# Two transformer blocks on one core: both feed-forward networks by a seven-product block scheme instead of plain products

## The chip, the core and the metric

The kernel runs on one NeuronCore of a Trainium2 chip. The core has a matrix engine (TensorE, PE in the profile, with its weight loads shown apart as PEld), a vector engine (VectorE, DVE), an activation engine (ScalarE, ACT), a general engine (GpSimd, POOL) and a queue that issues transfers (SyncE, SP). SBUF is the on-chip memory that all of them read; PSUM is where TensorE leaves its products. The metric is the device time of one execution in microseconds. Before the change it is 1985.58 us, the median of three runs (1983.51 to 1989.43).

## The reference

One batch of 512 tokens with 1024 features goes through two transformer blocks in float32. Only the feed-forward networks are touched by the change. They are

```
hffn = modulate(rmsnorm(x, g_norm2[l]), shift2, scale2)
a, u = jnp.split(jnp.einsum('bsd,df->bsf', hffn, w_ffn_in[l]), 2, axis=-1)
x = x + gate2[:, None, :] * jnp.einsum('bsf,fd->bsd', jax.nn.silu(a) * u, w_ffn_out[l])
...
h = rmsnorm_2(x, norm_ffn[l])
x = x + (jax.nn.silu(h @ w_ffn_gate[l]) * (h @ w_ffn_up[l])) @ w_ffn_down[l]
return rmsnorm_2(x, norm_final)
```

Each network has 2816 hidden features, so it holds a product of 512 x 1024 by 1024 x 5632 and one of 512 x 2816 by 2816 x 1024.

## The kernel before

Float32 accuracy on TensorE comes from a split: every operand is kept as a high part (rounded to the engine's fp32r type by a ScalarE copy) and a low part (the operand minus the high part, on VectorE), and every product is three matmuls, high by high, high by low and low by high (`mm3`, lines 159 to 162). Weights arrive by `weights` (lines 167 to 174): SP loads four row tiles of 256 columns (512 KB) into a `raw` tile, ScalarE writes `wh` (line 172), VectorE writes `wl` (line 173). There are three buffers of each, so loading and splitting run ahead of the matmuls by up to three steps.

A feed-forward network works in 11 stripes of 256 hidden columns (`ffn_hidden`). For each stripe `gemm` runs the gate columns and then the up columns for all 512 tokens: 8 row tiles, 2 column tiles of 128 and 3 matmuls, each streaming 512 columns. PSUM is read by ScalarE (sigmoid, line 869) and VectorE (lines 870 and 873), and the result is split again into the operand of the second product. The second product of the first block goes through `joint`: 22 row tiles by 8 column tiles, feature-major, with the residual update in line 790, the last columns by token halves. That of the second block is token-major: the weights are streamed and the hidden operand is loaded (lines 1352 to 1354), PSUM is started with the transposed residual, and the last norm closes it token tile by token tile (lines 1367 to 1381). The engines run their queues in order; a tile framework lays the buffers out, rotates them per tag, and adds the waits.

GpSimd has little to do in these stretches: it adds squares for the norms (line 799) and issues some spills. In other stretches it also adds and subtracts whole tiles (lines 649, 650, 733, 748), and for part of the second block it makes the low parts of weights (line 173, where `low_engine` is set to it).

## Time and profile before

| what | value |
|---|---|
| median of three runs | 1985.58 us (1983.51 to 1989.43) |
| span of the profiled execution | 1987.4 us |
| TensorE busy | 1919.9 us, 97% |
| VectorE busy | 1060.0 us, 53% |
| ScalarE busy | 732.1 us, 37% |
| GpSimd busy | 318.7 us, 16% |
| first feed-forward network, about | 882 to 1260 us of the span |
| second feed-forward network, about | 1596 us to the end |

The profiled execution has no time of its own beside its span of 1987.4 us, which lies inside the three runs' spread. A share of busy time is an average over the whole span; the stretches differ, and the views by window show each of them. A wait is time in which an engine sat idle before an instruction, with the instruction that released it behind the arrow. The granted clock is TensorE's clock as a share of 2.4 GHz.

### The profile page before, as it was taken

Reading aid. Unit: us, or ns where it says so; the run is one execution under the profiler, and the core shown is the slowest. Engines: PE = TensorE matmul, PEld = TensorE weight load, DVE = VectorE, ACT = ScalarE, POOL = GpSimd, SP = SyncE. Lnnn points to the kernel's source line nnn. Section 1 sums busy time; section 2 is a strip of 40 time slices with the busy share of each in tenths; the row PEclk is TensorE's granted clock in tenths of the full one; section 3 lists DMA queues with packets and bytes.
Section 4 is the critical chain, followed back from the end, with each engine's and each line's share of the span. In section 5 each row is a group of like instructions: output and inputs, shape, how many; then the busy total and the mean of one; then the engine's idle time right before and its main releaser. Section 6 shows DMA issues by size and latency. Waiting matters only on the chain.

```text
span 1987.4 us, 24615 instructions
## 1 busy us (share of the span) xinstructions
PE 1919.9 (97%) x9561; PEld 1574.0 (79%) x9561; DVE 1060.0 (53%) x1730; ACT 732.1 (37%) x1250; POOL 318.7 (16%) x357
## 2 busy tenths in 40 slices
PE   5899999999999999999999999979999999999998
PEld 4677777888989898888888888867877788888886
DVE  6777766645555555654343322587477653443222
ACT  3556654233332323333232223552255532222222
POOL 3322221102030302010000002242344200000000
PEclk7999999999999999999999999989899989999999
DMA  6612222443424243623333234232133123333222
GB/s 210 201 54 64 64 64 78 156 133 96 133 85 144 75 138 118 204 82 96 95 96 95 90 101 122 62 110 64 34 100 101 43 75 95 95 91 92 94 85 74
DMA packets 193521, 199.25 MB, mean 100 GB/s; under 512 B 9719, under 2 KB 178693, under 8 KB 193405
## 3 DMA queue, kind: packets, MB, share of 16 engines
q1 hardware_dynamic: 189920, 188.48, 30.9%
q0 software_dynamic: 3136, 9.08, 1.3%
q8 instruction: 75, 1.23, 0.3%
q14 instruction: 42, 0.34, 0.1%
q10 hardware_dynamic: 348, 0.13, 0.0%
HBM read 189.25 MB, written 9.99 MB: 100 GB/s over the span
## 4 chain that ended last, share of the span: by engine, by line
PE 88%; DVE 6%; ACT 2%; issue 2%; POOL 1%; DMA 1%; SPq 0%; POOLq 0%; DVEq 0%; ACTq 0%
PE ps_g L160 20%; PE ps_g L161 20%; PE ps_g L162 20%; PE ps_g L203 3%; PE ps_g L204 3%; PE ps_g L205 3%; PE ps_o L530 1%; PE ps_z L493 1%; DVE t L319 1%; PE ps_z L161 1%; PE ps_z L160 1%; PE ps_z L162 1%; PE ps_r L515 1%; PE ps_g L1354 1%; PE ps_g L1353 1%
## 5 line engine op out<-in xcount | busy, mean ns | idle before, releaser
L160 PE MATMUL ps_g<-p,wh 128*128 128x512 f32 (+1 forms) x1464 | 584.6, 402 | 11.3 <-ACT p L150 3.0
L161 PE MATMUL ps_g<-p,wh 128*128 128x512 f32 (+1 forms) x1464 | 577.2, 394 | 2.8 <-DVE p L405 2.8
L162 PE MATMUL ps_g<-p,wl 128*128 128x512 f32 (+1 forms) x1464 | 576.2, 394 | 0.0
L173 DVE TENSOR_TENSOR wl<-raw,wh 128x1024 fp32r<-128x1024 f32 (+1 forms) x262 | 325.9, 1244 | 450.8 <-ACT wh L172 449.7
L172 ACT CAST wh<-raw 128x1024 fp32r<-128x1024 f32 (+1 forms) x282 | 294.3, 1044 | 652.5 <-PE ps_g L161 373.1
L160 PEld LDWEIGHTS ps_g<-p,wh 128*128 128x128 f32 x1464 | 276.0, 189 | 83.8 <-issue 14.2
L161 PEld LDWEIGHTS ps_g<-p,wh 128*128 128x128 f32 x1464 | 277.8, 190 | 63.4 <-DVE p L405 3.6
L162 PEld LDWEIGHTS ps_g<-p,wl 128*128 128x128 f32 x1464 | 277.3, 189 | 63.6 <-issue 0.4
L203 PE MATMUL ps_g<-wh,p 128*128 128x256 f32 x512 | 150.4, 294 | 1.5 <-ACT wh L172 1.5
L204 PE MATMUL ps_g<-wl,p 128*128 128x256 f32 x512 | 146.1, 285 | 0.9 <-DVE wl L173 0.9
L205 PE MATMUL ps_g<-wh,p 128*128 128x256 f32 x512 | 145.9, 285 | 0.0
L160 PE MATMUL ps_g<-q,wh 128*128 128x512 f32 (+1 forms) x368 | 142.2, 389 | 0.0
L161 PE MATMUL ps_g<-q,wh 128*128 128x512 f32 (+1 forms) x368 | 141.7, 385 | 0.0
L162 PE MATMUL ps_g<-q,wl 128*128 128x512 f32 (+1 forms) x368 | 141.6, 385 | 0.0
L203 PEld LDWEIGHTS ps_g<-wh,p 128*128 128x128 f32 x512 | 98.9, 193 | 5.3 <-ACT wh L172 1.9
L204 PEld LDWEIGHTS ps_g<-wl,p 128*128 128x128 f32 x512 | 99.2, 194 | 1.7 <-DVE wl L173 1.1
L205 PEld LDWEIGHTS ps_g<-wh,p 128*128 128x128 f32 x512 | 99.1, 193 | 0.0
L160 PEld LDWEIGHTS ps_g<-q,wh 128*128 128x128 f32 x368 | 69.1, 188 | 15.9 <-issue 0.6
L162 PEld LDWEIGHTS ps_g<-q,wl 128*128 128x128 f32 x368 | 69.2, 188 | 15.1
L161 PEld LDWEIGHTS ps_g<-q,wh 128*128 128x128 f32 x368 | 69.2, 188 | 14.6 <-issue 0.2
L150 ACT CAST q<-t 128x512 fp32r<-128x512 f32 (+1 forms) x68 | 39.1, 581 | 87.4 <-DVE t L873 48.7
L319 DVE SCALAR_TENSOR_TENSOR adaacc<-raw,cact,adaacc 128x256 f32<-128x256 f32 x112 | 53.8, 481 | 27.9 <-DMA raw<-in_w_ada 26.1
(373 smaller groups left out, 2622.3 us busy)
## 6 DMA issues: line engine op xcount, KB each, us to landing
raw<-in_w_in SPq DMA_DIRECT2D x108, 512.0 KB, 3.6
raw<-in_w_ffn_in SPq DMA_DIRECT2D x44, 512.0 KB, 3.5
raw<-in_w_ada SPq DMA_DIRECT2D x32, 512.0 KB, 3.4
raw<-in_w_ffn_gate SPq DMA_DIRECT2D x22, 512.0 KB, 3.7
raw<-in_w_ffn_up SPq DMA_DIRECT2D x22, 512.0 KB
raw<-in_w_ffn_down SPq DMA_DIRECT2D x22, 512.0 KB, 3.6
raw<-in_w_ffn_out SPq DMA_DIRECT2D x19, 512.0 KB, 3.5
raw<-in_w_proj_ret SPq DMA_DIRECT2D x16, 512.0 KB, 3.3
```

What stands on the lines that cost most here:

```text
L150: nc.scalar.copy(hi, src)
L160: nc.tensor.matmul(ps, lh, rh, start=start, stop=False)
L161: nc.tensor.matmul(ps, lh, rl, start=False, stop=False)
L162: nc.tensor.matmul(ps, ll, rh, start=False, stop=stop)
L172: nc.scalar.copy(wh, raw)
L173: low_engine["e"].tensor_tensor(out=wl, in0=raw, in1=f(wh), op=ALU.subtract)
L203: nc.tensor.matmul(o, xh[:, ts], wh[:, i], start=k == 0 and t % 2 == 0, stop=False)
L204: nc.tensor.matmul(o, xh[:, ts], wl[:, i], start=False, stop=False)
L205: nc.tensor.matmul(o, xl[:, ts], wh[:, i], start=False, stop=k == KD - 1 and t % 2 == 1)
L319: nc.vector.scalar_tensor_tensor(out=acc, in0=w, scalar=c, in1=acc, op0=ALU.mult, op1=ALU.add)
L493: nc.tensor.matmul(z[:, 0:W], qs[h][r, ts], ks[h][1][r, 0:W], start=False, stop=True)
L515: nc.tensor.matmul(o, src, rhs[:, i * 128:i * 128 + 128], start=True, stop=True)
```

## The change

Both networks are computed by blocks. A block is a 2 x 2 arrangement: the tokens in two halves of 256, the rows of the weight in two halves (four row tiles each, three in the middle group of the second product), and the columns in two halves of 256. In place of 8 half-products per block there are 7 products of sums and differences of quarters; every product is 4 row tiles by 2 column tiles by 3 matmuls that stream 256 columns, 24 matmuls (18 in the middle group). In the first product the two column halves are a gate stripe and its up stripe, so a hidden stripe is one block, and the seven sums of the normed operand (`Operand`, the `S` tiles) are made once and serve all 11 stripes. The second product takes the hidden rows in three groups of 8, 6 and 8 row tiles with two blocks each; for every group seven `S` operands are made anew from the hidden tiles (`hidden_operand`, `sums`).

Per block four differences of weight quarters are made on GpSimd (`sub`: t1 to t4, line 913 of the changed kernel), and seven splits follow where plain products have four (lines 167 and 168). Three partial results are copied from PSUM by ScalarE, and three additions on VectorE put them together. The order of the products is woven over neighbouring blocks (`woven`), and each is prepared two steps ahead (`play`). The second block's second product is now token-major in this form, with its residual transposed during the hidden stripes. Part of SBUF is laid out twice: one set of tags in the mixing stages, another in the feed-forward networks, seven `raw` buffers in place of three among them.

```diff
-# microseconds of weight products traced after each stage of the latency-bound parts
+MIX = {"q": 36, "raw": 3, "wh": 3, "wl": 3}
...
+                return P.tile([128, T], dt, tag=tag, name=tag, bufs=SLOTS[tag])
+            return region["pool"].tile([128, T], dt, tag=tag, name=tag, bufs=region["slots"][tag])
...
+        class Operand:
...
...
+            def put(self, name, piece, src):
+                if name not in self.S:
+                    self.S[name] = [wtile("S", [128, self.kn, 256], F32R) for _ in range(2)]
+                a, n = self.at[piece], self.widths[piece]
+                hi, lo = (x[:, a:a + n] for x in self.S[name])
+                split(src, hi, lo)
...
+            def sums(self, piece, x11, x12, x21, x22, eng=None):
+                eng = eng or nc.gpsimd
+                s1, s2, s3, s4 = (self.temp(piece) for _ in range(4))
+                eng.tensor_tensor(out=s1, in0=x21, in1=x22, op=ALU.add)
+                eng.tensor_tensor(out=s2, in0=s1, in1=x11, op=ALU.subtract)
+                self.put(6, piece, s2)
+                nc.gpsimd.tensor_tensor(out=s3, in0=x11, in1=x21, op=ALU.subtract)
+                self.put(7, piece, s3)
+                self.put(5, piece, s1)
+                nc.gpsimd.tensor_tensor(out=s4, in0=x12, in1=s2, op=ALU.subtract)
+                self.put(3, piece, s4)
+                self.put(4, piece, x22)
...
+                self.kn = len(rows[0])
+                self.raw, self.w, self.ps, self.sb = {}, {}, {}, {}
...
+            def load(self, i, j):
+                t = wtile("raw", [128, self.kn, 256], F32)
+                w, c = self.cols[j - 1]
...
+            def sub(self, out, a, b):
+                nc.gpsimd.tensor_tensor(out=out, in0=a, in1=b, op=ALU.subtract)
+            def prep(self, i):
+                raw = self.raw
+                if i == 1:
+                    self.load(1, 1)
+                elif i == 2:
+                    self.load(2, 1)
+                    src = raw[2, 1]
+                elif i == 6:
+                    self.load(1, 2)
+                    self.load(2, 2)
+                    t1, t3, t4 = raw[1, 1], raw[1, 2], raw[2, 1]
+                    self.sub(t1, raw[1, 2], raw[1, 1])
+                    t2 = wtile("raw", [128, self.kn, 256], F32)
+                    self.sub(t2, raw[2, 2], t1)
+                    self.sub(t3, raw[2, 2], raw[1, 2])
+                    self.sub(t4, raw[2, 1], t2)
+                    self.T = {6: t2, 7: t3, 5: t1, 3: raw[2, 2], 4: t4}
+                    src = t2
+                else:
+                    src = self.T[i]
+                wh = wtile("wh", [128, self.kn, 256], F32R)
+                wl = wtile("wl", [128, self.kn, 256], F32R)
+                split(src, wh, wl)
+                self.w[i] = wh, wl
+            BANK = {1: "A", 6: "A", 5: "A", 3: "A", 2: "B", 7: "C", 4: "C"}
+            TAG = {"A": "g", "B": "z", "C": "r"}
...
+            def product(self, i):
...
+                wh, wl = self.w.pop(i)
+                sh, sl = self.X.S[i]
+                for n in range(2):
+                    o = ps[:, n * 256:n * 256 + 256]
+                    s = slice(n * 128, n * 128 + 128)
+                    for k in range(self.kn):
+                        st = first and n == 0 and k == 0
+                        sp = last and n == 1 and k == self.kn - 1
...
+                        else:
+                            nc.tensor.matmul(o, wh[:, k, s], sh[:, k], start=st, stop=False, skip_group_check=True)
+                            nc.tensor.matmul(o, wh[:, k, s], sl[:, k], start=False, stop=False, skip_group_check=True)
+                            nc.tensor.matmul(o, wl[:, k, s], sh[:, k], start=False, stop=sp, skip_group_check=True)
+                self.done.add(i)
+                self.after(i)
+            def after(self, i):
+                if i in (1, 6, 5):
+                    self.sb[i] = new("t")
+                    nc.scalar.copy(self.sb[i], self.ps["A"])
+                if i == 2:
+                    nc.vector.tensor_add(self.sb[1], self.ps["B"], self.sb[1])
+                    self.out(1, 1, self.sb[1])
+                if i in (5, 7) and {5, 7} <= self.done:
+                    nc.vector.tensor_add(self.sb[5], self.ps["C"], self.sb[5])
+                    self.out(2, 2, self.sb[5])
+                if i == 3:
+                    self.out(1, 2, self.ps["A"])
+                if i == 4:
+                    nc.vector.tensor_add(self.sb[6], self.ps["C"], self.sb[6])
+                    self.out(2, 1, self.sb[6])
...
+        def play(steps):
+            for b, i in steps[:2]:
+                b.prep(i)
+            for n, (b, i) in enumerate(steps):
+                if n + 2 < len(steps):
+                    c, j = steps[n + 2]
+                    c.prep(j)
+                b.product(i)
+                yield b, i
+        def woven(blocks):
+            steps = []
+            for n, b in enumerate(blocks):
+                if n == 0:
+                    steps += [(b, 1), (b, 2)]
+                steps += [(b, 6), (b, 7), (b, 5)]
+                if n + 1 < len(blocks):
+                    c = blocks[n + 1]
+                    steps += [(c, 1), (b, 3), (b, 4), (c, 2)]
+                else:
+                    steps += [(b, 3), (b, 4)]
+            return steps
...
+        X2, put2 = normed_operand()
-            for k in range(KD):
+            def make(k, out):
+                t = new("t")[:, 0:256]
+                nc.vector.scalar_tensor_tensor(out=t, in0=x2[k][:, HS[hf]], scalar=a2[:, k:k + 1], in1=R[:, 0:256],
+                                               op0=ALU.mult, op1=ALU.mult)
+                nc.scalar.activation(out, t, AF.Identity, bias=mod[:, 24 + k:25 + k])
+            put2(hf, make)
...
-        def ffn_hidden(w_a, ca, w_u, cu, X):
-            hid = []
-            for c in range(11):
...
+        GROUPS = (range(0, 4), range(4, 7), range(7, 11))
+        def ffn_hidden(wa, ca, wu, cu, X):
+            hid = {}
+            blocks = []
+            for s in range(11):
+                hold = {}
+                def out(i, j, c, s=s, hold=hold):
+                    if j == 1:
+                        g = new("t")
+                        nc.scalar.activation(g, c, AF.Sigmoid)
+                        (nc.vector if i == 1 else nc.gpsimd).tensor_tensor(out=c, in0=c, in1=g, op=ALU.mult)
+                    hold[i, j] = c
+                    if (i, 1) in hold and (i, 2) in hold:
+                        h = new("p")
+                        nc.vector.tensor_mul(h, hold[i, 2], hold[i, 1])
+                        hid[s, i] = h.rearrange("p (k n) -> p k n", n=256)
+                blocks.append(Block((range(0, 4), range(4, 8)), ((wa, ca + 256 * s), (wu, cu + 256 * s)), X, out))
+            steps = woven(blocks)
...
+            steps[:10] = [(b, 1), (b, 2), (c, 1), (c, 2), (b, 6), (b, 7), (b, 5), (c, 6), (b, 3), (b, 4)]
+            return hid, steps
...
+        def hidden_operand(g, hid):
+            X = Operand([2 if n is None else 1 for _, n in top])
+            def build(step):
+                for h in range(2):
+                    if step < 2:
+                        X.put(1 + step, h, get(1, (top, low)[step][h]))
+                    else:
+                        X.sums(h, get(1, top[h]), get(1, low[h]), get(2, top[h]), get(2, low[h]))
+            return X, rows, build
...
+        def ffn(hidden_steps, hid, w, out_of, tok=False, last=None):
...
+            for g in range(3):
+                X, rows, build = hidden_operand(g, hid)
+                for c in range(2):
+                    b = Block(rows, ((w, 512 * c), (w, 512 * c + 256)), X, out_of(g, c), tok)
+                    blocks.append(b)
+                    if c == 0:
+                        builds[b] = build
+            steps = woven(blocks[:4])
...
+            for b, build in builds.items():
+                run_at.setdefault(b.at[1] - 3, []).append((build, 0))
+                run_at.setdefault(b.at[2] - 3, []).append((build, 1))
+                run_at.setdefault(b.at[6] - 4, []).append((build, 2))
+            for n, _ in enumerate(play(all_steps)):
+                for build, step in run_at.get(n, ()):
+                    build(step)
...
-        joint(A["w_ffn_out"], KF, hid, x2, 40, [None, "g_final"], fin3)
+        def out_y(g, c):
+            def out(i, j, blk):
+                hs = HS[i - 1]
+                for e in range(2):
+                    n = 4 * c + 2 * (j - 1) + e
+                    nc.vector.scalar_tensor_tensor(out=x2[n][:, hs], in0=blk[:, e * 256:e * 256 + 256],
+                                                   scalar=mod[:, 40 + n:41 + n], in1=x2[n][:, hs], op0=ALU.mult, op1=ALU.add)
+                    if g < 2:
+                        continue
...
+        def out_final(g, c):
+            def out(i, j, blk):
+                v = y[i, c, j]
+                nc.vector.tensor_add(v, blk, v)
+                if g < 2:
+                    return
...
+                    o = 8 * (i - 1) + 4 * t + 2 * c + j - 1
+                    nc.scalar.activation(s, v[:, t * 256:t * 256 + 256], AF.Square, accum_out=sfin[:, o:o + 1])
...
+        hid, hidden_steps = ffn_hidden(A["w_ffn_gate_2"], 0, A["w_ffn_up_2"], 0, X4)
+        ffn(hidden_steps, hid, A["w_ffn_down_2"], out_final, True, beside)
```

In the order of the engines three places matter for the prediction. The first is VectorE in a hidden stripe. Before, in the second stripe of the first network, with `raw` the loaded weights, `wl` a low part, `ps_g` a product and `t` a working tile:

```order
L173 TENSOR_TENSOR wl_8495<-raw_8492,wh_8494 128x1024
L870 TENSOR_TENSOR t_8415<-ps_g_8349,t_8414 128x512
L173 TENSOR_TENSOR wl_8525<-raw_8522,wh_8524 128x1024
L873 TENSOR_TENSOR t_8399<-ps_g_8418,t_8399 128x512
L151 TENSOR_TENSOR p_8470<-t_8399,p_8469 128x512
L873 TENSOR_TENSOR t_8415<-ps_g_8419,t_8415 128x512
L173 TENSOR_TENSOR wl_8565<-raw_8562,wh_8564 128x1024
L151 TENSOR_TENSOR p_8487<-t_8415,p_8486 128x512
L173 TENSOR_TENSOR wl_8595<-raw_8592,wh_8594 128x1024
```

Now, in one stripe in the middle; raw_9003, 9096, 9128 and 9130 are the four quarters of this stripe's weights, raw_9133 its t2, raw_9234 and up belong to the next stripe, raw_9364 and 9359 are that one's t2 and t3:

```order
L168 TENSOR_TENSOR wl_9237<-raw_9234,wh_9236 128x1024
L168 TENSOR_TENSOR wl_9266<-raw_9130,wh_9265 128x1024
L168 TENSOR_TENSOR wl_9297<-raw_9096,wh_9296 128x1024
L978 TENSOR_TENSOR t_9293<-ps_r_9240,t_9293 128x512
L168 TENSOR_TENSOR wl_9330<-raw_9327,wh_9329 128x1024
L1066 TENSOR_TENSOR p_9357<-ps_g_9069,t_9094 128x512
L168 TENSOR_TENSOR wl_9369<-raw_9364,wh_9368 128x1024
L983 TENSOR_TENSOR t_9232<-ps_r_9240,t_9232 128x512
L168 TENSOR_TENSOR wl_9403<-raw_9359,wh_9402 128x1024
L1066 TENSOR_TENSOR p_9400<-t_9293,t_9232 128x512
L975 TENSOR_TENSOR t_9325<-ps_z_9406,t_9325 128x512
L168 TENSOR_TENSOR wl_9436<-raw_9234,wh_9435 128x1024
```

What was four low parts per stripe with PSUM reads between them is now seven low parts, and the hidden tile (p_9400) stands between the low parts of t3 (wl_9403) and of t1 (wl_9436).

GpSimd had next to nothing in the hidden stripes before (one instruction in each of the two windows shown below). Now its queue holds, per stripe, four differences and one multiplication, which belongs to the stripe before:

```order
L1062 TENSOR_TENSOR t_8770<-t_8770,t_8935 128x512
L913 TENSOR_TENSOR raw_9003<-raw_9128,raw_9003 128x1024
L913 TENSOR_TENSOR raw_9133<-raw_9130,raw_9003 128x1024
L913 TENSOR_TENSOR raw_9128<-raw_9130,raw_9128 128x1024
L913 TENSOR_TENSOR raw_9096<-raw_9096,raw_9133 128x1024
L1062 TENSOR_TENSOR t_9001<-t_9001,t_9166 128x512
```

The multiplication of t_9001, which the hidden tile p_9169 waits for, stands behind the four differences of the next stripe. On SP the four loads of a stripe now stand like this, with the second-half-column quarters (9128, 9130) right ahead of the first-half-column quarters of the next stripe (9234, 9327):

```order
L907 DMA raw_9096<-in_w_ffn_in 128x4x256
L907 DMA raw_9128<-in_w_ffn_in 128x4x256
L907 DMA raw_9130<-in_w_ffn_in 128x4x256
L907 DMA raw_9234<-in_w_ffn_in 128x4x256
L907 DMA raw_9327<-in_w_ffn_in 128x4x256
```

raw_9130 uses the buffer of the earlier stripe's second quarter and is therefore issued after that quarter's last split. The second place is the start of a group in the second product, on GpSimd (L880 to L886 are the sums of the hidden tiles, L913 the differences of weights):

```order
L913 TENSOR_TENSOR raw_10808<-raw_10805,raw_10626 128x1024
L913 TENSOR_TENSOR raw_10803<-raw_10805,raw_10803 128x1024
L880 TENSOR_TENSOR t_10725<-p_8539,p_8938 128x512
L881 TENSOR_TENSOR t_10726<-t_10725,p_8505 128x512
L883 TENSOR_TENSOR t_10727<-p_8505,p_8539 128x512
L886 TENSOR_TENSOR t_10728<-p_8895,t_10726 128x512
L880 TENSOR_TENSOR t_10753<-p_8707,p_9169 128x512
L913 TENSOR_TENSOR raw_10771<-raw_10771,raw_10808 128x1024
L881 TENSOR_TENSOR t_10754<-t_10753,p_8664 128x512
L883 TENSOR_TENSOR t_10755<-p_8664,p_8707 128x512
L886 TENSOR_TENSOR t_10756<-p_9126,t_10754 128x512
L1062 TENSOR_TENSOR t_10618<-t_10618,t_10841 128x512
```

Eight sums of hidden tiles stand between the differences of weights and the multiplication of the last stripe. The third place is VectorE at the same point, where `S` are the low parts of the new operand:

```order
L168 TENSOR_TENSOR wl_10774<-raw_10771,wh_10773 128x1024
L168 TENSOR_TENSOR S_10732<-t_10726,S_10731 128x512
L1066 TENSOR_TENSOR p_10801<-ps_g_10455,t_10480 128x512
L168 TENSOR_TENSOR S_10737<-t_10727,S_10736 128x512
L168 TENSOR_TENSOR wl_10813<-raw_10808,wh_10812 128x1024
L168 TENSOR_TENSOR S_10741<-t_10725,S_10740 128x512
L168 TENSOR_TENSOR S_10732<-t_10754,S_10731 128x512
L168 TENSOR_TENSOR S_10746<-t_10728,S_10745 128x512
L168 TENSOR_TENSOR S_10737<-t_10755,S_10736 128x512
L168 TENSOR_TENSOR S_10750<-p_8938,S_10749 128x512
L168 TENSOR_TENSOR S_10741<-t_10753,S_10740 128x512
L168 TENSOR_TENSOR S_10746<-t_10756,S_10745 128x512
```

Here low parts of the operand stand ahead of and behind the low part of the weight t2 (wl_10813), in a row; none of them was there before, when the second product took the hidden tiles as they were.

## Rows read from the trace of the kernel before

**Rows 1.** The page: span, and each engine's busy time.

```profile
span 1987.4 us, 24615 instructions
...
PE 1919.9 (97%) x9561; PEld 1574.0 (79%) x9561; DVE 1060.0 (53%) x1730; ACT 732.1 (37%) x1250; POOL 318.7 (16%) x357
```

**Rows 2.** Windows over both networks: length, busy us per engine (count), clock, DMA.

```profile
885.00:1105.00 220.00, 219.72 (x985) 178.69 (x984) 94.11 (x118) 65.94 (x88) 0.88 (x1) 1.00 0.32 96
1110.00:1230.00 120.00, 120.00 (x516) 96.71 (x515) 34.97 (x37) 31.79 (x40) 16.22 (x16) 1.00 0.34 105
...
1832.00:1965.00 133.00, 133.00 (x602) 108.20 (x601) 33.82 (x36) 28.74 (x35) 0.00 (x0) 1.00 0.27 83
```

**Rows 3.** Line 160, 1000 to 1010 us: 15 matmuls, min/median/max ns, first and last start.

```profile
L160 PE MATMUL ps_g<-p,wh x15: 395/396/396, 1000.0 to 1009.8; 128*128 128x512 f32 x15
```

**Rows 4.** Timeline of PE, 256 columns: first and last of 33 matmuls (start, length, ...).

```profile
869.74 0.28 PE L160 MATMUL ps_g<-q,wh 128*128 128x256 f32 x1
...
873.53 0.27 PE L162 MATMUL ps_g<-q,wl 128*128 128x256 f32 x1
```

**Rows 5.** Timeline of VectorE and GpSimd from 377.5 us.

```profile
378.10 0.68 DVE L648 TENSOR_TENSOR t<-ps_g,k 128x512 f32<-128x512 f32 x1
378.33 1.29 POOL L649 TENSOR_TENSOR t<-t 128x512 f32<-128x512 f32 x1 [10.76 <-DVE t L647]
378.70 2.01 DVE L173 TENSOR_TENSOR wl<-raw,wh 128x1024 fp32r<-128x1024 f32 x1
379.58 2.28 POOL L650 TENSOR_TENSOR t<-t 128x512 f32<-128x512 f32 x1
...
380.63 1.78 DVE L151 TENSOR_TENSOR q<-t,q 128x512 fp32r<-128x512 f32 x1
...
382.73 0.68 DVE L151 TENSOR_TENSOR q<-t,q 128x512 fp32r<-128x512 f32 x1
```

**Rows 6.** Timeline of GpSimd and VectorE from 1437 us.

```profile
1437.03 2.40 POOL L173 TENSOR_TENSOR wl<-raw,wh 128x1024 fp32r<-128x1024 f32 x1
...
1437.76 2.22 DVE L151 TENSOR_TENSOR q<-q 128x512 fp32r<-128x512 f32 x1 [1.73 <-ACT q L150]
```

**Rows 7.** Groups by form: engine, operation, shapes, count, busy us, mean ns.

```profile
L172 ACT CAST wh<-raw 128x1024 fp32r<-128x1024 f32 x277 | 290.8, 1050 | 634.1 <-PE ps_g L161 354.7 <-issue 173.8 <-PE ps_r L1354 39.4
L728 ACT COPY q<-ps_r 128x512 f32<-128x512 f32 x16 | 9.4, 587 | 12.0 <-PE ps_r L162 12.0
```

**Rows 8.** Timeline of VectorE alone: a low part, and a residual update of 256 columns.

```profile
869.07 1.22 DVE L173 TENSOR_TENSOR wl<-raw,wh 128x1024 fp32r<-128x1024 f32 x1
872.43 0.48 DVE L790 SCALAR_TENSOR_TENSOR p<-ps_g,mod,p 128x256 f32<-128x256 f32 x1 [2.13 <-PE ps_g L162]
```

**Rows 9.** The page, transfers: KB each, median us from issue to landing.

```profile
raw<-in_w_ffn_in SPq DMA_DIRECT2D x44, 512.0 KB, 3.5
...
p<-xspill SPq DMA_DIRECT2D x8, 256.0 KB, 5.4
```

**Rows 10.** Timeline of PE around an idle of 2.04 us.

```profile
60.79 0.61 PE L324 MATMUL ps_o<-ones,t 128*128 128x1 f32 x4 [2.04 <-DVE t L319]
...
61.57 0.39 PE L162 MATMUL ps_z<-p,wl 128*128 128x512 f32 x1
61.80 0.39 PE L160 MATMUL ps_z<-p,wh 128*128 128x512 f32 x1
```

**Rows 11.** Timeline of PE after an idle of 3.76 us.

```profile
1591.34 1.01 PE L268 MATMUL ps_o<-ones,t 128*128 128x1 f32 x4 [3.76 <-POOL t L799]
...
1592.58 0.41 PE L161 MATMUL ps_z<-p,wh 128*128 128x256 f32 x1
1592.79 0.41 PE L162 MATMUL ps_z<-p,wl 128*128 128x256 f32 x1
```

**Rows 12.** Timeline of the end: last matmul and last scaling on ScalarE.

```profile
1980.56 0.39 PE L1354 MATMUL ps_r<-wh,q 128*128 128x512 f32 x1
...
1982.58 0.72 ACT L1378 ACTIVATE t<-t,rfin 128x512 f32<-128x512 f32 x1 [0.90 <-POOL rfin L1377]
```

259 lines of the change are left out of this document (168 added, 91 removed).

## The prediction

> **What bounds the kernel now.** The first view is the page's line of busy times: TensorE is busy for 97% of 1987.4 us [rows 1]. That is an average, so the second view is the table by windows over the two networks: TensorE is busy all the time there, at its full clock of 2.4 GHz, VectorE about 43% in the hidden stripes and 25 to 29% in the second products, GpSimd almost never [rows 2]. So each network is bound by its matmuls and every other engine has room. The third view gives the price of a matmul. Fifteen starts of one line, three matmuls apart, span 9.8 us: 0.70 us for three, 233.3 ns for one of 512 columns [rows 3]. Thirty-three of 256 columns span 3.79 us: 118.4 ns [rows 4]. Two halves cost 1.5% more than one whole.
>
> The fourth view is the timeline where VectorE and GpSimd work at once, because the change makes them do so. A low part of 1024 columns takes 1.22 us alone [rows 8], but 2.01 beside a GpSimd addition: it ends 1.09 us after that addition's end. The next GpSimd addition, 1.29 alone, takes 2.28 and ends 1.15 after the low part; the next low part of 512, 0.68 alone, takes 1.78 and ends 0.55 after that [rows 5]. A GpSimd subtraction of 1024 columns takes 2.40, and a low part of 512 issued under it again ends 0.55 after it [rows 6]. These do not share, they take turns. A VectorE instruction with one input in PSUM is untouched (0.68, line 648) [rows 5]. So VectorE instructions with both inputs in SBUF and GpSimd's arithmetic are one queue, with these prices in turn: low part 1.09 (1024) and 0.55 (512), residual update of 256 about 0.35 (0.48 alone [rows 8], less the same 0.13), GpSimd 2.27 (1024, 2.40 less 0.13) and 1.15 (512).
>
> **The matmuls.** Per network, before: 11 x 96 + 528 = 1584 matmuls of 512, 369.6 us. After: 11 x 168 + 4 x 168 + 2 x 126 = 2772 of 256, 328.2 us. Both networks together save 83 us if nothing else ends later.
>
> **A hidden stripe.** Its products take 168 x 0.1184 = 19.9 us (before 96 x 0.2333 = 22.4). The common queue carries seven low parts (7.6), two VectorE products of 512 (1.1), four differences (9.1) and GpSimd's multiplication (1.15): 19.0 us. That alone would just fit, but the order makes a loop out of it. From the end of product 5 of a stripe: the copy out of PSUM (0.59) and the cast of t4 (1.05) [rows 7] bring 1.6. Then the low part of t4 finds GpSimd at t1 of the next stripe, whose load went out 2.8 us before the end, landed after 3.5 [rows 9] at 0.7 and holds until 3.1; the low part ends at 4.2. Only now is the buffer free into which the fourth quarter of the next stripe is loaded: 7.7. t2 needs it: 10.1. t3 follows at once and holds until 12.5, while the cast of t2 runs beside it; the low part of t2 ends at 13.6, and product 6 starts. Four products (11.4) lay between, so TensorE has waited 2.2. t4 holds until 15.9, the low part of t3 ends at 17.0: product 7, another 0.6. Then GpSimd's multiplication (18.1), the hidden tile behind it, a PSUM addition and the low part of t1, which is queued behind both (20.4): product 5, 0.6. It ends at 23.3; with the signals between engines I take 23.5. That is 1.1 over the old stripe, +24 for 22 stripes. ScalarE, 7 casts, 3 copies and 2 sigmoids of about 0.6, is busy 11 of these 23 and hides.
>
> The Trainium skill gives 262 cycles at the full clock for a 256-column matmul issued back to back (TensorE: Matmul & The Clock Gate, Back-to-back issue gap), 109 ns, where the row has 118.4; by that the loop, which holds one product, would be 0.2 shorter and the sum 5 us lower. The row decides.
>
> **The second product.** A group of eight row tiles is two blocks. VectorE: 14 low parts of weights (15.3), 14 of the operand (7.7), 12 residual updates with both inputs in SBUF (4.2). GpSimd: eight differences (18.2) and eight sums of hidden tiles (9.2). Together 54.5 us of common queue, against 39.8 of products and 44.8 before. The group of six: 41.9. All three: 151, and 12 additions of squares of 256 (half of a 512, about 0.7 each) 8: 159. In the second network the updates are three additions of 512 per block (2.7 less) and 12 multiplications with the gain take the squares' place: 157. Here the queue, not TensorE, is the bound: 316 against 2 x 123.2. It can't be full all the time: at the start of a group eight sums and a difference stand ahead of the multiplication that the last stripe's hidden tile needs, and products 6 and 7 wait for the low parts of the sums. From both sides: full, 316; with the hidden stripe's share (19.0 of 23.5, 81%), 390. I take 93%, near the full end because two queues with work waiting leave few gaps: 340, +94.
>
> **Start, end, layout.** Product 1 now needs the normed tiles of half the tokens (eight of about 0.4) and four low parts (0.6), 5.6 us, where one tile was enough; the last half-products of the step before cover 5.7 (48 matmuls) in the first network and 2.8 (24) in the second. Product 6 needs the other half: 3.2 for the norm and 12.7 of queue for sums (4 on each engine) and ten low parts, against four products, 11.4. Together 4.5 and 7.3: +12. After the last matmul there are now 6.4 us [rows 1, 12]; two additions, squares, and six scalings of about 0.45 on ScalarE (0.72 for 512 [rows 12]) make about 9.5: +3. At the four borders of the two layouts the next weights may have to wait for a buffer at the same place: between 0 and a load, a cast and a low part (5.8); I take 1 each, since a load that is early needs no cover: +4. The transposes of the residual are as many as before, inside TensorE's idle time, and their copies on ScalarE hide; merged tiles under another tag cost nothing, the same instructions stand there.
>
> **Sum.** 24 + 94 + 12 + 3 + 4 = +137 on the profiled 1987.4, 2124. The median of the runs is 1.8 below that span, so 2122.
>
> **Rivals.** (1) Faster: the common queue hides. If VectorE and GpSimd overlapped freely, a stripe would be its products (copy, cast, low part, load, t2, cast, low part are 11.2 against 11.4), the second products 109.4 each: -83 + 19, 1922. For it: all engines but TensorE have room [rows 2]. Against it: the turns are exact to a few hundredths [rows 5, 6], in these very operations. It decides in favour of faster only if the queue per stripe fell under some 15 us, since the second products lose by it anyway. Chance 0.09.
>
> (2) The queue is full and the loop is not: GpSimd or SP run further ahead than I read. Then stripes cost 19.9 each (-55), the second products 316 (+70), and with 19 for the rest the time is 2019. Against: the loop rests on the order of the queues, above all on the buffer of the fourth quarter. Chance 0.12.
>
> (3) Slower still, by loads and clock. Three loads now leave together at that quarter. Eight loads of 256 KB sent together landed after 5.4 us, one of 512 KB after 3.5 [rows 9]: up to 1.9 a stripe, +42. And TensorE idles 2.2 us per stripe: after 2.04 idle it went on at 0.23 us per 512 columns, 2.4 GHz [rows 10], after 3.76 at 0.21 per 256, 1.2 GHz [rows 11]. At 1.2 a product takes 5.1 instead of 2.84, which makes products 7 and 5 late by up to 1.7 each, +73. Half of both: 2180; all of it 2237. Chance 0.14. The skill has all transfers run on the same 16 DMA engines and interleave (DMA: Bandwidth & Descriptors, Issuing engines are not separate DMA queues), which speaks for the loads' part; by it alone the time would be 2164.
>
> (4) The gains and losses cancel, or waits of the new layouts put something else in front: within 0.3%, which is about what a measurement of this kernel can tell from no change. Chance 0.03.
>
> **Numbers.** The forecast has 0.62, alone about 2060 to 2165 (second products between full and 85%, a stripe between 22.5 and 24.5). The range 2015 to 2190 adds (2) and the nearer half of (3) and leaves out (1), (4) and the far half, under 0.2. Faster 0.09, same 0.03, slower 0.88.
>
> **What would show it.** Right: in the hidden stripes about 23.5 us from one block's product 5 to the next, low parts with a mean well over 1.22 us, GpSimd differences over 2.40, TensorE waiting longest for the low part or cast of t2; in the second products VectorE and GpSimd together without gaps, groups of 55 to 60 us, TensorE busy about 70%. The step fails if GpSimd differences run at 2.40 beside low parts at 1.22, or if stripes take 20 us. It is wrong altogether if VectorE and GpSimd overlap freely; then the time is under 1985.

## The result, and the profile after

The changed kernel takes 2126.19 us (median of four runs, 2121.94 to 2128.38) where the kernel before takes 1985.13 in the same runs: a ratio of 1.070 (95% interval 1.067 to 1.072). The forecast was 2122. The total is right, but partly by luck: as the stretches show, large terms behind it were wrong with opposite signs. The ratios of the experiments below are against executions of the kernel before that were timed beside each of them (medians 1987.39 to 1991.94).

The page's first lines of the changed kernel, which answer to [rows 1]:

```profile
span 2124.3 us, 30121 instructions
...
PE 1912.0 (90%) x11791; PEld 1688.2 (79%) x11791; DVE 1495.4 (70%) x2017; ACT 921.4 (43%) x1552; POOL 812.6 (38%) x583
```

TensorE falls from 97% to 90% of a longer span, and GpSimd's busy time grows by half a millisecond. The view by windows of the same kernel (columns as in [rows 2]: length, busy us of PE, PEld, DVE, ACT, POOL with counts, granted clock, DMA) over five hidden stripes, the first second product, the mixing stage between the networks, and the other second product:

```profile
990.00:1095.00 105.00, 102.40 (x844) 101.38 (x843) 98.03 (x66) 48.77 (x60) 65.02 (x26) 1.00 0.33 101
1151.00:1310.00 159.00, 120.41 (x846) 115.44 (x845) 127.61 (x141) 73.43 (x116) 100.23 (x60) 0.83 0.21 65
1326.09:1688.86 362.77, 330.45 (x1718) 269.54 (x1718) 227.31 (x512) 167.41 (x351) 127.27 (x111) 0.91 0.25 74
1946.00:2112.00 166.00, 119.49 (x865) 116.05 (x865) 131.23 (x131) 74.20 (x129) 96.83 (x58) 0.83 0.18 57
```

In the hidden stripes TensorE hardly waits; in the second products it is busy three quarters of the time, at a mean granted clock of 0.83 where [rows 2] had 1.00. And the mixing stage, which the change doesn't touch, is longer than in the kernel before, where the same view has

```profile
1259.74:1600.31 340.57, 318.30 (x1688) 257.70 (x1687) 223.26 (x503) 160.38 (x340) 119.47 (x105) 0.93 0.26 76
```

So I cut every trace at the same five marks: the first matmul of the first network, the first matmul of the mixing stage behind it, the first matmul of the second network, the end of the last matmul, and the end. The stretches in us (the e-numbers are the experiments below):

| kernel | ahead | network 1 | between | network 2 | end | median us |
|---|---|---|---|---|---|---|
| before | 882.0 | 377.8 | 340.6 | 380.6 | 6.4 | 1985.13 |
| after | 889.1 | 437.0 | 362.8 | 425.1 | 10.3 | 2126.19 |
| e1, differences on VectorE | 883.1 | 396.8 | 360.7 | 382.5 | 10.6 | 2036.51 |
| e2, all on VectorE | 884.7 | 391.7 | 360.3 | 381.4 | 10.3 | 2031.81 |
| e3, layout taken up later | 884.2 | 438.9 | 348.9 | 431.0 | 10.2 | 2115.01 |
| e4, fourth quarter elsewhere | 886.5 | 434.9 | 361.6 | 424.3 | 10.2 | 2125.78 |
| e5, t2 computed twice | 890.3 | 457.4 | 365.8 | 448.3 | 10.3 | 2174.48 |
| e6, blocks in hidden stripes only | 889.5 | 390.1 | 362.0 | 379.1 | 11.2 | 2033.53 |
| e7, combined | 883.2 | 374.2 | 350.0 | 370.7 | 11.2 | 1990.50 |
| e8, fixed buffers | 878.7 | 372.9 | 354.8 | 373.2 | 9.7 | 1985.63 |
| e9, sums on VectorE | 892.0 | 424.5 | 361.8 | 407.7 | 10.3 | 2099.82 |
| e10, last halves apart | 877.8 | 371.3 | 348.0 | 373.6 | 8.7 | 1980.94 |

Before to after: +7.1 ahead, +59.2, +22.2, +44.5, +3.9, together 137.

**A hidden stripe.** PE's timeline of the changed kernel: the first matmul of product 5 in two neighbouring stripes.

```profile
1050.03 0.38 PE L964 MATMUL ps_g<-S,wh 128*128 128x256 f32 x1 [0.52 <-ACT t L973]
...
1070.99 0.38 PE L964 MATMUL ps_g<-S,wh 128*128 128x256 f32 x1 [0.52 <-ACT t L973]
```

A stripe takes 20.97 us, not 23.5, six times in a row in the first network and five in the second (the two or three ahead of these take 20.2 to 20.9). TensorE waits 0.5 of it, for a copy out of PSUM and not, as forecast, for the split of t2. Its seven products take 2.88 each (24 matmuls, 120.0 ns one). The groups by form of the window 990 to 1095, which answer to [rows 5, 6, 8], show the turns:

```profile
L168 DVE TENSOR_TENSOR wl<-raw,wh 128x1024 fp32r<-128x1024 f32 x36 | 84.7, 2363 | 1.2 <-ACT wh L167 1.2
L913 POOL TENSOR_TENSOR raw<-raw 128x1024 f32<-128x1024 f32 x21 | 59.5, 2845 | 32.1 <-DVE wl L168 25.7 <-issue 6.1
```

A low part lasts 2.36 us on average (alone 1.22), a difference 2.85 (alone 2.40): the time above that is waiting inside the instruction. Laid over each other, the intervals of VectorE's operations with two SBUF inputs and of GpSimd's arithmetic cover 19.7 of the 20.97 us. The forecast of that queue was 19.0.

**Why the loop didn't bind.** VectorE, SP and GpSimd one stripe long (start, length): the low part of a stripe's t3; then three of the four loads of that round; then t1 and t2 of the next stripe.

```profile
1065.16 1.21 DVE L168 TENSOR_TENSOR wl<-raw,wh 128x1024 fp32r<-128x1024 f32 x1
1066.39 0.37 SPq L907 DMA_DIRECT2D raw<-in_w_ffn_in  x1
1071.80 2.40 POOL L913 TENSOR_TENSOR raw<-raw 128x1024 f32<-128x1024 f32 x1 [4.28 <-DVE wl L168]
1074.28 3.27 POOL L913 TENSOR_TENSOR raw<-raw 128x1024 f32<-128x1024 f32 x1
1075.31 0.37 SPq L907 DMA_DIRECT2D raw<-in_w_ffn_in  x1
1078.66 0.37 SPq L907 DMA_DIRECT2D raw<-in_w_ffn_in  x1
```

t2 begins 0.08 us after t1 ends, so its fourth quarter is there. That load left at 1066.39, right behind the low part of t3 (1066.37), 7.9 us ahead of t2; landing takes 3.4. The loads leave one by one, each behind a low part that ends, at 1064.70, 1066.39, 1075.31 and 1078.66.

**The start of a group.** From the first group of the first network: GpSimd's first sums of hidden tiles and the difference between them, VectorE's first low part of a sum, and what TensorE waits for.

```profile
1147.55 1.28 POOL L880 TENSOR_TENSOR t<-p 128x512 f32<-128x512 f32 x1
1148.91 1.30 POOL L881 TENSOR_TENSOR t<-t,p 128x512 f32<-128x512 f32 x1
...
1151.41 1.73 POOL L886 TENSOR_TENSOR t<-p,t 128x512 f32<-128x512 f32 x1
...
1154.77 3.34 POOL L913 TENSOR_TENSOR raw<-raw 128x1024 f32<-128x1024 f32 x1
1158.07 1.71 POOL L881 TENSOR_TENSOR t<-t,p 128x512 f32<-128x512 f32 x1
```

```profile
1150.89 1.11 DVE L168 TENSOR_TENSOR S<-t,S 128x512 fp32r<-128x512 f32 x1 [5.56 <-ACT S L167]
```

```profile
1155.94 0.58 PE L966 MATMUL ps_g<-S,wl 128*128 128x256 f32 x1 [2.34 <-DVE wl L168]
1160.48 0.58 PE L964 MATMUL ps_g<-S,wh 128*128 128x256 f32 x1 [3.31 <-ACT S L167]
```

GpSimd works without a gap from 1147.55 to 1162.7 while VectorE and ScalarE wait for it and TensorE for them; the first group of the second network starts with 11 us of TensorE idle. Over 1151 to 1310 us the common queue is occupied 152 of 159 us (95%), over the other second product 152 of 167 (91%). That leaves two readings of the same trace: the queue's sum sets the pace, or the chain at each group start does. The experiments try to part them.

### The profile page after: what moved, and what is told of

The parts are those of the page before. It is cut to its first block, busy times and chain, and to the rows that moved or that the text cites. A ratio compares the mean times of both kernels' runs of the same rounds, so it can differ in the third digit from the quotient of the medians.

```text
span 2124.3 us, 30121 instructions
## 1 busy us (share of the span) xinstructions
PE 1912.0 (90%) x11791; PEld 1688.2 (79%) x11791; DVE 1495.4 (70%) x2017; ACT 921.4 (43%) x1552; POOL 812.6 (38%) x583
## 3 DMA queue, kind: packets, MB, share of 16 engines
q1 hardware_dynamic: 194048, 188.48, 28.8%
## 4 chain that ended last, share of the span: by engine, by line
PE 34%; DVE 9%; POOL 7%; issue 5%; ACT 2%; DMA 1%; ACTq 0%; POOLq 0%; DVEq 0%; SPq 0%
PE ps_g L964 4%; POOL raw L913 4%; PE ps_g L966 4%; PE ps_g L965 4%; DVE wl L168 3%; DVE S L168 3%; PE ps_g L177 2%; PE ps_r L964 2%; PE ps_r L965 2%; PE ps_g L179 2%; PE ps_r L966 2%; PE ps_g L178 2%; PE ps_o L287 1%; POOL t L880 1%; PE ps_z L966 1%
## 5 line engine op out<-in xcount | busy, mean ns | idle before, releaser
L168 DVE TENSOR_TENSOR wl<-raw,wh 128x1024 fp32r<-128x1024 f32 (+2 forms) x242 | 446.4, 1853 | 61.6 <-ACT wh L167 60.8
L913 POOL TENSOR_TENSOR raw<-raw 128x1024 f32<-128x1024 f32 (+1 forms) x136 | 375.4, 2770 | 220.7 <-DVE wl L168 149.1
L167 ACT CAST wh<-raw 128x1024 fp32r<-128x1024 f32 (+2 forms) x242 | 243.3, 1010 | 234.0 <-PE ps_g L965 76.6
L177 PE MATMUL ps_g<-p,wh 128*128 128x512 f32 (+2 forms) x792 | 324.1, 413 | 18.3 <-ACT wh L189 10.9
L178 PE MATMUL ps_g<-p,wh 128*128 128x512 f32 (+2 forms) x792 | 316.3, 399 | 3.8 <-DVE p L424 3.8
L179 PE MATMUL ps_g<-p,wl 128*128 128x512 f32 (+2 forms) x792 | 314.7, 398 | 0.4 <-POOL wl L190 0.4
L964 PE MATMUL ps_g<-S,wh 128*128 128x256 f32 x880 | 258.6, 294 | 29.7 <-ACT t L973 13.8
L966 PE MATMUL ps_g<-S,wl 128*128 128x256 f32 x880 | 256.2, 292 | 12.8 <-DVE wl L168 12.7
L965 PE MATMUL ps_g<-S,wh 128*128 128x256 f32 x880 | 255.6, 290 | 1.1 <-DVE S L168 1.1
L964 PEld LDWEIGHTS ps_g<-S,wh 128*128 128x128 f32 x880 | 175.1, 199 | 35.2 <-ACT t L973 18.3
L177 PEld LDWEIGHTS ps_g<-p,wh 128*128 128x128 f32 (+1 forms) x792 | 152.9, 194 | 61.5 <-issue 12.5
L966 PEld LDWEIGHTS ps_g<-S,wl 128*128 128x128 f32 x880 | 174.8, 199 | 15.2 <-DVE wl L168 15.2
L178 PEld LDWEIGHTS ps_g<-p,wh 128*128 128x128 f32 (+1 forms) x792 | 153.6, 194 | 32.8 <-DVE p L424 4.3
L965 PEld LDWEIGHTS ps_g<-S,wh 128*128 128x128 f32 x880 | 175.2, 199 | 1.9 <-DVE S L168 1.9
```

The source lines that it names most:

```text
L167: nc.scalar.copy(hi, src)
L168: nc.vector.tensor_sub(lo, src, f(hi))
L177: nc.tensor.matmul(ps, lh, rh, start=start, stop=False)
L178: nc.tensor.matmul(ps, lh, rl, start=False, stop=False)
L179: nc.tensor.matmul(ps, ll, rh, start=False, stop=stop)
L913: nc.gpsimd.tensor_tensor(out=out, in0=a, in1=b, op=ALU.subtract)
```

## The experiments

**e1: the four differences of weights on VectorE.**

```diff
-                nc.gpsimd.tensor_tensor(out=out, in0=a, in1=b, op=ALU.subtract)
+                nc.vector.tensor_tensor(out=out, in0=a, in1=b, op=ALU.subtract)
```

> The four differences of weight quarters per block run on VectorE in place of GpSimd; nothing else changes. Theory A (VectorE's operations with two SBUF inputs and GpSimd's arithmetic are one queue, and in the second products that queue sets the pace): a difference costs the queue about 1.13 us in place of 2.27. In the second products the queue was occupied 151 of 159 us in the changed kernel; it holds 22 full-size differences per network, so it falls by 25 to about 126 and each second product by about 26 us. In the hidden stripes the queue falls from 19.7 to 15, below TensorE's 20.2; the stripes go from 20.97 to 20.2 to 20.7 us. Low parts fall back to 1.22 us wherever GpSimd is idle. Total 2126 - 52 - 10 = about 2064 us. Theory B (the pauses at the group starts are a latency chain of eight sums on GpSimd, and the differences only run in its shadow): the second products lose at most the one difference that stands inside each chain, about 2 us per group; 2126 - 12 - 5 = about 2109 us. Theory C (the engines only slow each other's memory access and VectorE is short of time itself): moving work to the busier engine makes it slower than 2126 us.

Measured 2036.51 us, 1.0235 of before (1.020 to 1.027) and 90 less than the changed kernel. The same windows and form in its trace, stripes and first second product:

```profile
990.00:1095.00 105.00, 105.00 (x878) 105.00 (x877) 87.84 (x90) 52.37 (x63) 8.88 (x5) 1.00 0.33 101
1134.40:1276.60 142.20, 123.11 (x922) 119.09 (x920) 124.88 (x163) 68.15 (x109) 44.93 (x38) 0.92 0.26 80
```

```profile
L168 DVE TENSOR_TENSOR wl<-raw,wh 128x1024 fp32r<-128x1024 f32 x37 | 45.2, 1220 | 7.7 <-ACT wh L167 7.7
```

VectorE has four instructions more per stripe and is busy 10 us less: low parts are back at 1220 ns. TensorE has no pause left in the stripes: they take 20.16 us in the first network and 20.59 in the second, where transposes of the residual stand among the products. The second products fall from 171.7 and 168.0 us to 142.1 and 132.4. Theory A holds, with more than its price (65 us came off the second products where 52 were expected); B, which allowed 12 there, and C fall.

**e2: all of it on VectorE.** Besides e1's edit, the sums and the multiplication:

```diff
-                eng = eng or nc.gpsimd
+                eng = eng or nc.vector
...
-                        (nc.vector if i == 1 else nc.gpsimd).tensor_tensor(out=c, in0=c, in1=g, op=ALU.mult)
+                        nc.vector.tensor_tensor(out=c, in0=c, in1=g, op=ALU.mult)
```

> Differences of weights, sums of hidden tiles and the multiplication with the sigmoid all run on VectorE; GpSimd keeps only the additions of squares and the final multiplications. Theory A (one queue): beside the differences the sums cost 0.6 in place of 1.15 us, another 12 us of queue per network, but all of VectorE's own work in a second product is then about 130 us, which becomes the bound against TensorE's 111; about 2045 us in all, 10 to 20 under the run with the differences alone. Theory B (latency chain at the group starts): eight sums in a row take 5 us in place of 14, so each group start loses 8 us, 48 in all; about 2060 us while the run with the differences alone stays near 2109.

2031.81 us (1.021 of before, 1.0175 to 1.024): five less than e1, where A expected 10 to 20 less and B nearly 50 less. This is nearer to A, but half of its step at most. Against e1 the hidden stages (the stripes with their start) are 7.8 and 5.4 us shorter and the second products 2.8 and 4.2 us longer: VectorE by itself is now busy for nearly all of the first 87 us of the first second product, and for 87% of the whole of it:

```profile
1128.30:1170.00 41.70, 34.97 (x276) 34.77 (x275) 40.11 (x55) 19.16 (x27) 0.00 (x0) 0.92 0.25 77
1170.00:1215.00 45.00, 40.55 (x315) 39.94 (x314) 44.29 (x74) 24.68 (x41) 0.00 (x0) 0.92 0.30 94
1128.30:1273.20 144.90, 121.04 (x921) 118.41 (x919) 126.11 (x184) 70.02 (x112) 15.53 (x21) 0.89 0.25 78
```

**e9: the sums alone on VectorE**, differences on GpSimd as in the changed kernel (the edit is the first of e2, and the same in the two other sums).

> The changed kernel with the sums of hidden tiles on VectorE alone; the differences of weights stay on GpSimd. Theory A (one queue sets the pace of the second products): a sum of 512 columns costs the queue 0.6 in place of 1.15 us, 22 full-size sums per network make 12 us each, so 2126 - 24 = about 2100 us. Theory B (the chain of eight sums on GpSimd is what each group start waits for): the chain goes from about 14 to 5 us, six group starts win 8 us each, about 2078 us.

2099.82 us (1.057 of before, 1.054 to 1.061): A's 2100, not B's 2078. The networks are 12.5 and 17.4 us shorter, where the queue was to save 12 each. But this run doesn't test B. On VectorE the eight sums stand among low parts and are no sooner done; the first and the last of the first group:

```profile
1142.43 2.29 DVE L880 TENSOR_TENSOR t<-p 128x512 f32<-128x512 f32 x1
1158.63 0.68 DVE L886 TENSOR_TENSOR t<-p,t 128x512 f32<-128x512 f32 x1
```

From the first to the last they take 16.9 us here, where GpSimd in the changed kernel took 15.1 (1147.55 to 1162.69); over the six groups 9.4 to 16.9 against 10.7 to 16.1. What speaks against B is e1. There GpSimd, rid of the differences, takes 14.8 us for the first group's eight sums and 24 to 27 us in the groups behind it, but the first group's begin 26 us ahead of the second product in place of 3.5, and TensorE's idle time in the two second products falls from 39.5 and 46.5 us to 19.1 and 19.5:

```profile
1108.60 1.30 POOL L880 TENSOR_TENSOR t<-p 128x512 f32<-128x512 f32 x1
1121.10 2.26 POOL L886 TENSOR_TENSOR t<-p,t 128x512 f32<-128x512 f32 x1
```

So TensorE waited not for the length of the sums but for GpSimd's being late with them. How much of that was GpSimd's own work ahead of them, and how much the turns it had to wait for, these runs don't separate.

**e5: t2 computed twice**, to see whether the stripes are at the brink.

```diff
                     self.sub(t2, raw[2, 2], t1)
+                    if isinstance(self.rows[0], range):
+                        self.sub(t2, raw[2, 2], t1)
```

> In the hidden stripes GpSimd computes t2 twice in a row, into the same place; nothing else changes and the result is the same. Theory A (in the stripes of the changed kernel the common queue of VectorE's two-input operations and GpSimd is occupied 19.7 of 20.97 us, at the brink): one more turn of 2.27 us does not fit; a stripe takes 22 to 23 us in place of 20.97, about 18 stripes are longer, and the time is 2145 to 2165 us. Rival (GpSimd is busy for 52 of 84 us there and has room, VectorE only waits beside it): the extra instruction runs in GpSimd's idle time and the stripes stay at 21.0 us, 2126 us.

2174.48 us, 48 more than the changed kernel. Product 5 of two neighbouring stripes:

```profile
1087.08 0.38 PE L966 MATMUL ps_g<-S,wh 128*128 128x256 f32 x1 [0.52 <-ACT t L975]
...
1110.23 0.38 PE L966 MATMUL ps_g<-S,wh 128*128 128x256 f32 x1 [0.52 <-ACT t L975]
```

These two are 23.15 us apart, 2.18 more, for one more turn of 2.27: nearly all of it shows. The two networks are 20.4 and 23.2 us longer, about 2 us for each of the 22 stripes; the other 4 us lie in the stretches ahead and between. The measured time is above the range of theory A, for which I let only 18 stripes grow. GpSimd's idle third of the stripe was no room.

**e4: the load of the fourth quarter in another place of the order.**

```diff
                     self.load(2, 1)
+                    if self.early:
+                        self.load(2, 2)
...
+                blocks[-1].early = s >= 2
```

> In the hidden stripes from the third on, the fourth weight quarter of a stripe is loaded after the second one in place of ahead of the next stripe, so that by the order in which buffers come free it takes the buffer of the preceding stripe's t4, as the prediction assumed for the changed kernel; the arithmetic is the same. Theory (the stripes of the changed kernel take 20.97 and not 23.5 us only because that load leaves early, behind the low part of t3): a stripe now takes 23 to 24 us, 17 stripes are 2 to 3 us longer each, and the time is about 2170 us. Rival (the buffer has nothing to do with it, the queue at 94% is the bound either way): stripes stay at 21.0 us and the time at 2126.

2125.78 us, stripes of 20.97 us: no change. But the edit missed its aim: in its program the quarter took the buffer of t2, not of t4, and its loads leave as early as before. So this run tells nothing about a late load, and no other run makes it late. That the load is early in the changed kernel is read from its trace alone.

**e3: the second layout later.** The networks' layout is taken up only in the norm behind the output product (the same edit ahead of the first network):

```diff
-        lay_out(FFN)
...
         def fin4(hf, st):
+            if hf == 0:
+                lay_out(FFN)
```

> The second layout of SBUF is taken up only when the norm after the output product begins, so that the output product's weights use the buffers of the mixing stage; everything else as in the changed kernel. Theory (the border of the layouts held back the output product of the second block, whose products filled TensorE's gaps in the attention before the change): the stretch from the end of the first network to the start of the second one, 362.8 us against 340.6 before, gets back about 10 us, and the stretch ahead of the first network 3 to 5 us; some of it returns as waits of the first hidden weights. Total about 2111 us. Rival (those stretches are longer because TensorE comes out of a second product with pauses, and runs at 1.2 GHz there): the time stays within 3 us of 2126.

2115.01 us, 11 less than the changed kernel and near the theory's 2111. The stretch between goes from 362.8 to 348.9:

```profile
1323.12:1671.97 348.85, 322.88 (x1717) 262.87 (x1717) 225.58 (x514) 167.23 (x351) 119.40 (x107) 0.93 0.25 77
```

Where it was lost: the end of the attention, in the changed kernel and, at the same place, in the kernel before:

```profile
1626.00:1648.00 22.00, 16.37 (x77) 12.54 (x78) 11.88 (x39) 14.82 (x43) 0.50 (x1) 0.86 0.23 81
```

```profile
1549.00:1571.00 22.00, 22.00 (x120) 17.24 (x121) 12.38 (x40) 14.10 (x43) 0.84 (x1) 1.00 0.08 25
```

Before, products of the output projection stood between the short matmuls of the attention there; with the new layout ahead of them their weights had no buffers yet, TensorE paused and its clock fell (0.86 against 1.00). The wait for the norm ahead of the second network grew as well: 3.76 us before [rows 11], 6.77 in the changed kernel, 2.55 in e3. The networks themselves become 2 and 6 us longer in e3.

**e6: blocks in the hidden stripes only.** The second products take all eight half-products of the same tiles; its core:

```diff
+            def product(self, q):
+                r, j = q
+                wh, wl = self.w.pop(q)
+                for i in (1, 2):
+                    if r == 1:
+                        self.ps[i] = psum("zr"[i - 1])
+                    sh, sl = self.X.S[i, r]
...
+                    if r == 2:
+                        self.out(i, j, self.ps[i])
```

> The block scheme stays in the hidden stripes as it is in the changed kernel, with GpSimd's differences; the second products are computed with all eight half-products from the same tiles (four weight quarters, each split once, no differences, no sums; PSUM is added to the residual directly). TensorE then has 1056 matmuls of 256 columns per second product, 127 us. Theory A (the second products lose by the common queue, which without differences and sums holds 4 low parts per block and 8 low parts of the operand per group, under 20 us of 46): they run at TensorE's pace, 127 to 130 us in place of 172 and 168; the hidden stripes stay at 20.97; time 2035 to 2050 us. Rival (what costs there is the start of each group, where new operands must be split before TensorE can go on): about 10 us per group remain, 2090 us or more.

2033.53 us (1.024 of before, 1.020 to 1.028), just under A's 2035 to 2050. Windows in both second products:

```profile
1139.80:1275.00 135.20, 135.20 (x1130) 135.11 (x1128) 61.10 (x96) 42.69 (x70) 19.74 (x28) 1.00 0.27 86
1915.00:2015.00 100.00, 100.00 (x835) 100.00 (x835) 38.98 (x47) 27.72 (x52) 9.91 (x12) 1.00 0.18 58
```

TensorE never pauses there, at its full clock, through the group starts too: with a seventh more matmuls in the second products the networks are 47 and 46 us shorter. So the seven-product form pays in the hidden stripes at most, where one set of operand sums serves eleven blocks.

**e7, e8, e10: towards a faster version.** e7 joins e2's hidden stripes, e6's second products and e3's layout; e8 keeps the weights' buffers in place through both layouts and closes the last product by token tiles; e10 does the last column half for 256 tokens after the other:

```diff
+            steps[-2:] = [(b, (1, 2, 1)), (b, (2, 2, 1)), (b, (1, 2, 2)), (b, (2, 2, 2))]
```

> Hidden stripes by the block scheme with all arithmetic on VectorE, second products with eight half-products, and the second layout taken up only at the norm. By the parts measured so far: 884 us to the first network, 238 to 246 us of hidden stripes and 127 to 130 us of second product in each network, 345 to 349 us between them, 8 to 10 us at the end: 1970 to 1995 us, so level with the kernel before or a little faster. It would be faster by 20 us or more only if the mixing stage gets back to 340 us because TensorE comes into it without pauses.

> As the combined version, with two more edits: the buffers of weights (three raw, three high, three low parts) keep their places through both layouts, only four more raw buffers belong to the networks' layout, and the last product is closed token tile by token tile. If the waits of about 3 us for the first weights behind each border and the late first products of the mixing stage come from the buffers' places, the stretch between the networks goes from 350 to 343 to 346 us, and the end from 11.2 to about 8 us: 1979 to 1985 us, level with the kernel before or up to 0.4% faster. Rival (those microseconds come from the norm at the border, which has to run ahead of everything there): no change against the combined version, 1990 us.

> As the version with fixed buffers, but the last column half of the last block is done for the first 256 tokens completely and then for the other 256, so that the norm of the first half has 5.8 us of products beside it in place of 2.9. If the norm at the border is what the mixing stage waits for, the stretch between the networks goes from 354.8 to about 350 us and the end by up to 1 us: 1980 to 1985 us. Rival (the second half's norm alone decides): no change, 1986 us.

e7: 1990.50 us, 1.002 of before (1.0003 to 1.004). e8: 1985.63, 1.000 (0.998 to 1.002), between its theory's 1979 to 1985 and its rival's 1990. In its profiled execution the stretch ahead is 4.5 shorter than in e7, and the one between is not (350.0 and 354.8). But that execution took 1991.09 us, 5.5 over e8's median, so a few us between its stretches and e7's can't be read: what is shown is that the stretch between did not fall to the 343 to 346 that the buffers' places were to give, not that their places cost nothing. e10: 1980.94 us, 0.996 of before (0.9945 to 0.998), less than half a per cent faster than the kernel before, with 348.0 between the networks. It is 4.7 us under e8 by the medians, as expected if the norm, which now has twice the products beside it, was what the mixing stage waited for.

## Why the total was right and three of its terms were not

Cut by the prediction's own terms (us against before; the first two products of each second product lie inside the hidden stage, so 5.8 is taken from one and added to the other):

| term | forecast | measured | from |
|---|---|---|---|
| 22 stripes | +24 | -31.5 | 20.97 against 22.4 |
| start and end of the hidden stages | +12 | +31 | 256.2 and 251.4 in all, less 11 stripes each; before 254.5 and 253.6 |
| second products | +94 | +100.8 | 177.3 + 173.7 against 123.3 + 126.9 |
| borders and mixing stage | +4 | +32.8 | 7.1 ahead, 3.5 and 22.2 between |
| end | +3 | +3.9 | 10.3 against 6.4 |
| sum | +137 | +137.0 | |

The errors of the five terms are -55.5, +19, +6.8, +28.8 and +0.9 us, and they cancel. That the sum is met to the microsecond is luck; only the second products and the end were forecast for what they are. The first two rows go together, since their border is drawn by taking 20.97 for every stripe.

**The matmuls**: right; 120.0 ns one in the stripes, where 118.4 was taken [rows 4].

**The hidden stripe**: wrong, by 2.5 us each. The step that failed is "Only now is the buffer free into which the fourth quarter of the next stripe is loaded". I had counted the seven buffers round in a fixed turn; so the sentence on raw_9130 in the section on the change is wrong too. The program gives each new tile the buffer that was released first: t2 gets the buffer of t1, the fourth quarter that of t3, and its load leaves 7.9 us ahead of its use. With it fall "three loads now leave together" and the 2.2 us of idle per stripe on which rival 3 stood; the clock in the stripes is 1.00. The queue itself was right (19.0 forecast, 19.7 found), and e5 shows that the stripe is at its limit; e1, that without GpSimd's differences the stripe is TensorE's. The 0.6 us that the forecast had ahead of product 5 is there too (0.5), behind GpSimd's multiplication, the hidden tile and the PSUM addition that it named; a sigmoid, a cast and the copy on ScalarE end it.

**The second products**: right in size, and in cause as far as these runs go. Forecast were 159 and 157 us of queue at 93%, 340; measured are 351 us, with the queue occupied 95% and 91% of the two windows above and 90% of each second product to its end. The cause is borne out by three runs: in the changed kernel, e9 and e1 the second products take 132 to 172 us, but the queue is occupied for 87 to 91% of them each time. e6 takes the differences and sums away, and with them nearly all of the loss. Beside GpSimd's differences a low part takes 2363 ns on average, without them 1220. The Trainium skill says (SBUF — State Buffer, SBUF: two separate sides) that GpSimd and a VectorE operation with two SBUF inputs hold one pair of ports in turn, each for a whole instruction, without sharing; the trace agrees. The Trainium skill's ratio between GpSimd and VectorE for an elementwise operation on two inputs is about 1.96 (GPSIMD Engine Reference, Elementwise — side-by-side cycle accounting); here it is 2.40 to 1.22 us, 1.97 [rows 6, 8]. Together these two say that GpSimd can't relieve VectorE of such work; e1, 90 us faster, agrees.

**Start**: too small. I priced the waits of products 1 and 6; the trace of the first network also has product 7 waiting 8.45 us in pieces for its weights and its operand. No run divides this further.

**Borders**: the step that failed is "at the four borders ... between 0 and a load, a cast and a low part". The border held back a whole product that used to fill another stage's pauses; the order of instructions showed it, since the output projection's matmuls have left the attention's end there, but the prediction looked at it only inside the networks. e3 gets back 13.9 of 22.2 between the networks and 4.9 of 7.1 ahead. The remaining 8 may partly be the norm (e10, which gives it cover, is 4.7 us faster than e8); how much of the changed kernel's own 8 that is stays open.

**Rivals**: 1 (free overlap) is excluded by the turns. 2 had the stripes nearly right (19.9 against 20.97), but took the second products at 316 us, where 351 were measured, and 19 us for starts, borders and end together, where it was 68. 3 did not occur in the stripes. How much of the second products' loss is the lower clock of 0.83 and how much the pauses themselves was not separated: every run that took pauses away raised the clock as well (0.92 in e1's first second product, 1.00 in e6's).

## What to carry to other kernels

Fewer matmuls bought with elementwise work are a gain only if the elementwise queue has room; here VectorE's operations on two SBUF tiles and GpSimd's arithmetic counted as one queue, and a piece on GpSimd cost that queue double (2.40 us alone for 1024 columns, 1.22 on VectorE [rows 6, 8]). The block scheme paid where its operand sums are used eleven times (e7's networks take 374.2 and 370.7 us, 377.8 and 380.6 before), not where they are made anew for two blocks. And check a right total term by term: read from issue times which buffer a load waits for, and compare the order of instructions also in stages that the change does not touch.

## What the runs showed of the hardware that was not expected

Moving 136 instructions from the idler to the busier engine made VectorE itself less busy: in the stripes from 98.0 to 87.8 of 105 us (e1), because the time inside its instructions was waiting. VectorE can be busy for 97% of a stretch of 87 us (40.11 and 44.29 us in e2's second product) while TensorE keeps 87%, so the forecast's 93% is no ceiling within a stretch; over a whole second product no run here had the queue occupied for more than 91%.
